# Moving the load of u in a state-space stage: from the start of its own batch to right behind the outputs that free its buffer

## The chip, the cores and the metric

The kernel runs on one core of a Trainium2 chip. The metric is the device time of one execution in microseconds (us); lower is better. Times of a kernel before and after a change are compared as ratios with an interval.

The core has a matrix engine (TensorE, PE in the profile; its weight loads are listed as PEld), a vector engine (VectorE, DVE), a scalar engine (ScalarE, ACT), GpSimd (POOL), and SyncE (SP), which here only issues transfers to and from memory. Each engine works through its own list of instructions in the order in which the list was written. An instruction that has to wait for another engine holds up everything behind it in its own list.

## The reference, cut to what matters

The reference is a two-layer trunk over 1024 time steps and 1024 channels, all in float32. Layer 0 computes one projection of the normalised input and splits it into `u`, a gate, `q`, `k`, `v` and a second gate. `u` goes through a diagonal complex state-space layer ("S5"), `q`, `k`, `v` through chunkwise retention; both are gated, joined and projected back. Layer 1 is a gated convolution module. The change lies in the state-space layer, which in the reference is, for each of 64 groups of 16 channels and 64 states:

```
bu_re = einsum('tbgh,gnh->tbgn', u_c, bb_re)
bu_im = einsum('tbgh,gnh->tbgn', u_c, bb_im)
pr, pim, zr, zi = lax.associative_scan(
    _complex_affine_combine, (a_r, a_i, bu_re, bu_im), axis=0)
...
y = (einsum('tbgn,ghn->tbgh', xr, cre)
     - einsum('tbgn,ghn->tbgh', xi, cim)
     + dsk * u_c)
```

## The kernel before, in words

The input projection is done in blocks of 128 output channels. Eight blocks (`u_block`) make `u` and write it to memory in a layout that puts 8 neighbouring time steps and 16 channels on the 128 partitions. Sixteen blocks (`gate_block`, nb = 8 to 23) make the two gates; each is two halves of 24 matmuls of 128x512 (L200 to L202), scaled out of PSUM by VectorE (L393), passed through Silu by ScalarE (L394) and stored (L397).

The state-space layer is cut into 8 batches, B = 0 to 7, of 8 groups each, which are interleaved with the 16 gate blocks, two blocks to a batch. This document writes v(B), y(B), U(B) and so on for the instructions of one batch. A batch consists of:

- `s5_tables(B)`: GpSimd makes tables (18 operations, L766 to L768). For B > 1 it calls `s5_w2(B)`, which loads four tables, PTr, PTi, BTr and BTi (256 KB each, L799 and L802), and lets VectorE make the two weight tiles W2r and W2i of the batch from them, in six operations (L806 to L811; the last of W2r is L810, of W2i L811). For B = 0 and 1 the weights come from TensorE transposes that ScalarE copies (L859). Each of these tiles has one buffer.
- `s5_states(B)`: loads `U`, the batch's part of u, 512 KB (L850); TensorE multiplies it with W2r and W2i (L868, called v here); VectorE turns the result, runs two scans (L883) and makes the states S (L894, L895). Beside that, TensorE and ScalarE make a kernel matrix (kp L902 and L903, Kg L905 and L906, its transpose kt L908) which goes through memory (k_d L912, Wd L915) into the weights W1 (L917).
- `s5_out(B)`: TensorE multiplies W1 with U (L932) and W3 with S (L938, both called y here); ScalarE copies the result (L942), which is stored (y_d, L944).

`U` has two buffers, so the load of batch B+1 has to wait until the L932 matmuls of batch B-1 have read theirs. As the code is written, `s5_out(B - 1)` comes between the two gate blocks of batch B, and `s5_tables(B + 1)` after the second one.

The transfers are issued by SyncE in one list. A line of `s5_w2` ties the four table loads to the load of U: `issue_after(x)` adds an edge that keeps every instruction of the block, on the engine of x, behind x in that engine's list.

```
with self.tc.issue_after(self.u_load.ins):
    for c, (pt, bt) in enumerate(((ptr, btr), (pti, bti))):
        nc.sync.dma_start(pt[:]..., ...)
        nc.sync.dma_start(bt[:]..., ...)
```

`self.u_load` is whichever load of U was written last when `s5_w2` is called. Before the change, at `s5_tables(B + 1)` that is the load of U(B).

The order of each engine's list is set by a planner when the kernel is built. It walks a timeline that it reckons with its own durations, and gives each engine, among the instructions that are ready by that reckoning, the one that comes first in the code. An instruction can thus go far ahead of its place in the code (the loads of U(0) and U(1) are issued one behind the other), but the list that results is fixed, whatever the chip then does.

Of the kernel before, what the change touches and what calls it, by code (L numbers as in the profile page):

```python
# [11 lines left out]
F32 = mybir.dt.float32  # L12
# [7 lines left out]
P = 128  # L20
# [50 lines left out]
class Trunk:  # L71
# [191 lines left out]
    def layer0_front(self, st):  # L263
        tc, nc, A = self.tc, self.nc, self.A
# [36 lines left out]
        for kb in range(KB):  # L301
            t = xt[kb] = ev.tile([P, T], F32, name=f"x_{kb}", tag="xin", bufs=8)
            g = self.vec(V_NG0, kb)
# [66 lines left out]
        def u_block(nb):  # L370
            ut = uv.tile([P, 8, P], F32, name=f"ut_{nb}", tag="ut", bufs=2)

            def evac(h, ps):
                r = self.R[:, h * HALF:(h + 1) * HALF]
                o = ut[:, ::-1, h * 64:(h + 1) * 64].rearrange("p j (a m) -> p j a m", a=LANES)

                with self.tc.issue_after(self.u_evac[0].ins) if nb == 1 else nullcontext():
                    self.u_evac[nb] = nc.vector.tensor_tensor(
                        o, ps[:].rearrange("p (m j a) -> p j a m", j=8, a=LANES),
                        r.rearrange("p (a m j) -> p j a m", j=8, a=LANES), op=ALU.mult)  # L380
            if nb < 3:
                for h in range(2):
                    evac(h, (u01 + [u2])[nb][h])
            else:
                scaled(nb, self.wnext(f"u{nb}"), f"u{nb}", evac)
            nc.sync.dma_start(self.u_d[nb].rearrange("j h g m -> (h g) j m"), ut[:])

        def gate_block(nb, w, dst):
            gt = uv.tile([P, T], F32, name=f"gt_{nb}", tag="ut", bufs=2)

            def evac(h, ps):
                c = slice(h * HALF, (h + 1) * HALF)
                nc.vector.tensor_tensor(nat(gt[:, c]), un(ps[:]), nat(self.R[:, c]), op=ALU.mult)  # L393
                nc.scalar.activation(gt[:, c], gt[:, c], AF.Silu)  # L394
            scaled(nb, w, f"g{nb}", evac)
            k = nb % 8
            nc.sync.dma_start(dst[k * P:(k + 1) * P], gt[:])  # L397
# [12 lines left out]
        self.s5 = self.pool("s5w", 1, stack=st)  # L410
        for nb in range(5, 8):
            u_block(nb)
        self.s5_tab, self.s5_back, self.s5_last = {}, {}, None
        self.s5_turned()
        self.s5_tables(0)
        for nb in range(8, 24):
            B = (nb - 8) // 2
            if nb % 2 == 0:
                self.s5_states(B)
            gate_block(nb, self.wnext(f"g{nb}"), self.gs_d if nb < 16 else self.gr_d)  # L420
            if nb % 2 == 0 and B:
                self.s5_out(B - 1)
            if nb % 2 and B < 7:
                self.s5_tables(B + 1)
        self.s5_out(7)
# [388 lines left out]
    def s5_tables(self, B):  # L814
# [24 lines left out]
            nc.scalar.mul(R8[:, q, :], self.m01[:], self.r8[:, 4 * B + q:4 * B + q + 1])  # L839
        self.s5_tab[B] = Mr, Mi, W3, Tc, Ts, R8, self.s5_w2(B) if B > 1 else None  # L840

    def s5_states(self, B):
        nc, w = self.nc, self.s5
        gp, v = nc.gpsimd, nc.vector
        q0 = 4 * B
        Mr, Mi, W3, Tc, Ts, R8, W2 = self.s5_tab.pop(B)


        U = w.tile([P, 8, P], F32, name=f"U_{B}", tag="U", bufs=2)
        self.u_load = nc.sync.dma_start(U[:], self.u_d[B].rearrange("j h g m -> (j h) g m"))  # L850


        first, W2 = W2 is None, W2 or []
        for nm, M in (("r", Mr), ("i", Mi)) if first else ():
            ps = self.bank(f"w2{nm}_{B}")
            for q in range(4):
                nc.tensor.transpose(ps[:, q * P:(q + 1) * P], M[:, q, :], self.ident[:])
            t = self.big(f"W2{nm}_{B}", f"W2{nm}", 1)
            nc.scalar.copy(t[:].rearrange("p q n -> p (q n)"), ps[:])  # L859
            W2.append(t)  # L860

        V = []
        for c in range(2):
            ps = self.bank(f"v{c}_{B}")
            for q in range(4):
                for g2 in range(2):
                    r = slice(64 * g2, 64 * g2 + 64)
                    nc.tensor.matmul(ps[r, q * P:(q + 1) * P], W2[c][:, q, r], U[:, 2 * q + g2, :],  # L868
                                     start=True, stop=True)
            V.append(ps)  # L870
        fl = lambda t: t[:].rearrange("p q n -> p (q n)")

        tc, ts = fl(Tc), fl(Ts)
        vr, vi = V[0][:], V[1][:]
        t2, t4 = (fl(self.big(f"m{i}_{B}", "tmpV", 4)) for i in range(2))
        v.tensor_tensor(t2, vi, ts, op=ALU.mult)
        v.tensor_tensor(t4, vr, ts, op=ALU.mult)
        v.tensor_tensor(vr, vr, tc, op=ALU.mult)
        v.tensor_tensor(vi, vi, tc, op=ALU.mult)
        v.tensor_tensor(vr, vr, t2, op=ALU.add)  # L880
        v.tensor_tensor(vi, vi, t4, op=ALU.subtract)
        for z in (vr, vi):
            v.tensor_tensor_scan(z, fl(R8), z, 0.0, op0=ALU.mult, op1=ALU.add)  # L883

        S = w.tile([P, 2, 4, P], F32, name=f"S_{B}", tag="S", bufs=1)
        c1 = lambda t: t[:, :, 1:P]
        c0 = lambda t: t[:, :, 0:P - 1]
        zr, zi = (z.rearrange("p (q n) -> p q n", q=4) for z in (vr, vi))
        t2, t3 = (self.big(f"d{i}_{B}", "tmpV", 4) for i in range(2))
        v.tensor_tensor(c0(t2), c0(zi), c0(Ts), op=ALU.mult)  # L890
        v.tensor_tensor(c0(t3), c0(zr), c0(Ts), op=ALU.mult)
        v.tensor_tensor(c0(zr), c0(zr), c0(Tc), op=ALU.mult)
        v.tensor_tensor(c0(zi), c0(zi), c0(Tc), op=ALU.mult)
        v.tensor_tensor(c1(S[:, 0]), c0(zr), c0(t2), op=ALU.subtract)  # L894
        v.tensor_tensor(c1(S[:, 1]), c0(zi), c0(t3), op=ALU.add)  # L895
        v.memset(S[:].rearrange("p c q m -> p (c q) m")[:, :, 0:1], 0.0)


        kp = self.bank(f"kp_{B}")
        for q in range(4):  # L900
            o = kp[q * 32:(q + 1) * 32, :P]
            nc.tensor.matmul(o, self.cbr[:, q0 + q, :], Mr[:, q, :], start=True, stop=False)  # L902
            nc.tensor.matmul(o, self.cbni[:, q0 + q, :], Mi[:, q, :], start=False, stop=True)  # L903
        Kg = w.tile([P, P], F32, name=f"Kg_{B}", tag="Kg", bufs=1)
        nc.scalar.copy(Kg[:, 16:], kp[:, 16:P])  # L905
        v.tensor_tensor(Kg[:, :16], kp[:, :16], self.dd[:, B, :], op=ALU.add)  # L906
        kp = self.bank(f"kt_{B}")
        nc.tensor.transpose(kp[:, :P], Kg[:], self.ident[:])  # L908
        Kt = w.tile([P, P], F32, name=f"Kt_{B}", tag="Kg", bufs=1)
        nc.scalar.copy(Kt[:], kp[:, :P])  # L910

        nc.sync.dma_start(self.k_d[B, 112:], Kt[:])  # L912
        Wd = w.tile([P, 8, P], F32, name=f"Wd_{B}", tag="yb", bufs=1)
        kd = self.k_d[B]
        nc.sync.dma_start(Wd[:], bass.AP(tensor=kd.tensor, offset=kd.offset, ap=[[P, P], [16 * P, 8], [1, P]]))  # L915
        W1 = w.tile([P, 8, P], F32, name=f"W1_{B}", tag="W1", bufs=1)
        nc.scalar.copy(W1[:].rearrange("p g (i h) -> p i g h", i=8), Wd[:].rearrange("p i (g h) -> p i g h", g=8))  # L917
        self.s5_back[B] = U, W1, W3, S

    def s5_out(self, B):  # L920


        nc = self.nc
        U, W1, W3, S = self.s5_back.pop(B)
        yb = self.s5.tile([P, 8, P], F32, name=f"yb_{B}", tag="yb", bufs=1)
# [3 lines left out]
        def products():  # L929
            for q in range(4):  # L930
                for g2 in range(2):
                    yield nc.tensor.matmul(ps[g2][:, cols(q)], W1[:, 2 * q + g2, :], U[:, 2 * q + g2, :],  # L932
                                           start=q == 0, stop=False)
# [993 lines left out]
```

## Time and profile before

| | |
|---|---|
| median of 3 runs | 1144.9 us (1144.89 to 1146.61) |
| the profiled execution, its time | 1147.62 us |
| the profiled execution, span from first to last instruction | 1145.8 us |
| mean granted TensorE clock in it | 0.994 |
| state-space stage with the gate blocks | about 83 to 320 us of the span |
| U loads issued | 83.3 (two), 139.2, 170.6, 198.3, 227.7, 255.5, 283.2 us |
| v starts, B = 0 to 7 | 102.2, 126.6, 149.4, 176.9, 204.4, 232.5, 260.1, 289.1 us |
| W2i finished by VectorE, B = 2 to 7 | 146.0, 168.9, 196.6, 226.0, 253.8, 281.5 us |

A row of the timeline gives the start and the duration in us, the engine (with a q for an instruction that issues a transfer), the line of the code, the operation, the tile written and the tiles read, and how many instructions are merged into the row. In brackets stands how long the engine had been idle before it and what ended that. A row of the waits gives who waited for whom, the total, the number of times and the longest. A row of the windows gives a stretch of the span and, for each engine, how long it was busy in it. Matmuls of the gate blocks start 0.216 us apart when nothing holds them up; their duration of 0.38 us overlaps the next.

### The profile page before, as it was taken

The page shows a single profiled execution, that of the slowest core. Times are in us where ns is not written, and L with a number is a line of the kernel's source. Part 1 is how long each engine was busy: PE and PEld are TensorE (multiplying, and loading weights), DVE is VectorE, ACT ScalarE, POOL GpSimd, SP SyncE. Part 2 cuts the span into 40 slices and gives each one's busy share as a digit, 9 for nine tenths or more (in the row PEclk, how much of TensorE's full clock was granted, in tenths as well). Part 3 has the DMA queues.
Part 4 walks back from the last instruction along what each step waited for, and adds up shares of the span by engine and source line. Part 5 has one row for each costly group of instructions (what it writes and reads, how often), then busy time and mean ns, then how long its engine had stood idle before and what let it go on. Part 6 is the DMA issues. An engine that isn't in the chain of part 4 may idle for free.

```text
span 1145.8 us, 17197 instructions
## 1 busy us (share of the span) xinstructions
PE 1123.9 (98%) x6286; PEld 983.4 (86%) x6286; DVE 853.5 (74%) x1464; ACT 488.2 (43%) x719; POOL 657.7 (57%) x448
## 2 busy tenths in 40 slices
PE   9999999999999999999999999999999999999997
PEld 7888888888887888999887888888888888888787
DVE  6975798888417369596669632599999899999844
ACT  6423232223223321414446423545545676444674
POOL 2059999999235445333475111589544568678563
PEclk9999999999999999999999999999999999999999
DMA  9345355555487766858998998666778655357865
GB/s 352 113 129 159 128 166 177 162 175 177 154 256 247 285 199 211 297 182 308 382 375 295 321 321 285 191 232 203 247 249 298 238 177 173 120 188 248 287 226 193
DMA packets 117638, 261.46 MB, mean 228 GB/s; under 512 B 10673, under 2 KB 42289, under 8 KB 116913
## 3 DMA queue, kind: packets, MB, share of 16 engines
q1 hardware_dynamic: 117552, 260.36, 67.5%
q8 instruction: 49, 0.80, 0.3%
q14 instruction: 37, 0.30, 0.1%
HBM read 181.48 MB, written 74.65 MB: 224 GB/s over the span
## 4 chain that ended last, share of the span: by engine, by line
PE 34%; DVE 8%; DMA 7%; issue 2%; POOL 2%; ACT 1%; SPq 1%; POOLq 0%; ACTq 0%; DVEq 0%
DVE cv L1534 5%; PE mm_wo L202 5%; PE mm_wo L201 5%; PE mm_wo L200 5%; PE mm_b L201 2%; PE mm_b L202 2%; PE mm_b L200 2%; PE mm_a L202 2%; PE mm_a L201 2%; PE mm_a L200 2%; PE mm_oc L202 2%; PE mm_oc L201 1%; PE mm_oc L200 1%; DMA wf_glu<-w_glu 1%; DMA t_d<-th 1%
## 5 line engine op out<-in xcount | busy, mean ns | idle before, releaser
L1534 DVE SCALAR_TENSOR_TENSOR cv<-u,convw,cv 128x512 f32<-128x512 f32 x398 | 273.0, 749 | 6.6 <-ACT cv L1513 4.6
L1507 POOL TENSOR_TENSOR tp<-tp,tp 128x512 f32<-128x512 f32 x64 | 83.2, 1299 | 33.7 <-ACT tp L1506 32.7
L200 PE MATMUL mm_g<-xh,wh_g 128*128 128x512 f32 x256 | 98.9, 386 | 0.0
L201 PE MATMUL mm_g<-xl,wh_g 128*128 128x512 f32 x256 | 97.3, 380 | 0.0
L202 PE MATMUL mm_g<-xh,wl_g 128*128 128x512 f32 x256 | 97.2, 380 | 0.0
L437 POOL TENSOR_TENSOR s1q<-s1q,s1q 128x512 f32<-128x512 f32 x12 | 17.6, 1466 | 79.8 <-ACT s1q L432 79.8
L1506 ACT ACTIVATE tp<-u,convw 128x512 f32<-128x512 f32 x64 | 45.4, 718 | 35.5 <-POOL tp L1507 34.8
L200 PEld LDWEIGHTS mm_g<-xh,wh_g 128*128 128x128 f32 x256 | 48.4, 189 | 8.6 <-issue 1.2
L202 PEld LDWEIGHTS mm_g<-xh,wl_g 128*128 128x128 f32 x256 | 48.4, 189 | 6.9
L201 PEld LDWEIGHTS mm_g<-xl,wh_g 128*128 128x128 f32 x256 | 48.4, 189 | 6.8 <-issue 0.4
L190 POOL TENSOR_TENSOR wl_v<-wf_v,wh_v 128x1024 fp32r<-128x1024 f32 x12 | 31.0, 2593 | 36.4 <-ACT wh_v L189 36.4
L190 POOL TENSOR_TENSOR wl_glu<-wf_glu,wh_glu 128x1024 fp32r<-128x1024 f32 x14 | 34.3, 2447 | 29.9 <-ACT wh_glu L189 29.9
L200 PE MATMUL mm_oc<-zh,wh_woc 128*128 128x512 f32 (+1 forms) x144 | 51.3, 367 | 0.0
L202 PE MATMUL mm_oc<-zh,wl_woc 128*128 128x512 f32 (+1 forms) x144 | 51.0, 357 | 0.1
L201 PE MATMUL mm_oc<-zl,wh_woc 128*128 128x512 f32 (+1 forms) x144 | 51.1, 356 | 0.0
L201 PE MATMUL mm_u<-xl,wh_u 128*128 128x512 f32 x128 | 48.4, 381 | 0.7 <-DVE xl L316 0.7
L200 PE MATMUL mm_wo<-ysh,wh_wos 128*128 128x512 f32 x128 | 48.9, 382 | 0.0
L200 PE MATMUL mm_g<-h1h,wh_cg 128*128 128x512 f32 x128 | 48.9, 382 | 0.0
L201 PE MATMUL mm_b<-h1l,wh_cb 128*128 128x512 f32 x128 | 48.7, 381 | 0.1
L202 PE MATMUL mm_b<-h1h,wl_cb 128*128 128x512 f32 x128 | 48.7, 380 | 0.0
L201 PE MATMUL mm_wo<-ysl,wh_wos 128*128 128x512 f32 x128 | 48.5, 379 | 0.0
L202 PE MATMUL mm_wo<-ysh,wl_wos 128*128 128x512 f32 x128 | 48.5, 379 | 0.0
(526 smaller groups left out, 3622.9 us busy)
## 6 DMA issues: line engine op xcount, KB each, us to landing
wf_g<-w_ab SPq DMA_DIRECT2D x16, 512.0 KB
wf_wos<-w_out SPq DMA_DIRECT2D x16, 512.0 KB
wf_wor<-w_out SPq DMA_DIRECT2D x16, 512.0 KB
wf_cb<-w_c SPq DMA_DIRECT2D x16, 512.0 KB
wf_ca<-w_c SPq DMA_DIRECT2D x16, 512.0 KB
wf_woc<-w_out_c SPq DMA_DIRECT2D x16, 512.0 KB
wf_v<-w_v SPq DMA_DIRECT2D x12, 512.0 KB
wf_cg<-w_c SPq DMA_DIRECT2D x11, 512.0 KB
```

The lines of the kernel that those rows point to most:

```text
L190: self.low_made = lo[i].tensor_tensor(wl[:].rearrange(fl)[:, c], wf[:, c], h.bitcast(F32), op=ALU.subtract)
L200: nc.tensor.matmul(ps, wh[:, kb, :], xh, start=start, stop=False, **more)
L201: nc.tensor.matmul(ps, wh[:, kb, :], xl, start=False, stop=False, **more)
L202: self.last_mm = nc.tensor.matmul(ps, wl[:, kb, :], xh, start=False, stop=stop, **more)
L437: nc.gpsimd.tensor_tensor(a, a, sq[:], op=ALU.add)
L1506: nc.scalar.mul(sk[:], u[:, k:k + HALF], cw[:, nb, k:k + 1])
L1507: gp.tensor_tensor(s0[:], s0[:], sk[:], op=ALU.add)
L1534: v.scalar_tensor_tensor(dst[:], *tap, accs_[i][:], op0=ALU.mult, op1=ALU.add)
```

## The change

The load of U leaves `s5_states` and becomes a function of its own. For B = 0 and 1 it is called at the start of the batch, as before. For B = 2 to 7 it is called right behind `s5_out(B - 2)`, one gate block and one `s5_tables` earlier in the code. The buffers, the transfer and all computation stay the same. Because `self.u_load` is now set earlier, `s5_w2(B)` finds the load of U(B) in it, where it found that of U(B-1) before.

```
-        self.s5_tab, self.s5_back, self.s5_last = {}, {}, None
+        self.s5_tab, self.s5_back, self.s5_last, self.s5_us = {}, {}, None, {}
         self.s5_turned()
         self.s5_tables(0)
         for nb in range(8, 24):
             B = (nb - 8) // 2
             if nb % 2 == 0:
+                if B < 2:
+                    self.s5_load(B)
                 self.s5_states(B)
             gate_block(nb, self.wnext(f"g{nb}"), self.gs_d if nb < 16 else self.gr_d)
             if nb % 2 == 0 and B:
                 self.s5_out(B - 1)
+                if B < 7:
+                    self.s5_load(B + 1)
             if nb % 2 and B < 7:
                 self.s5_tables(B + 1)
         self.s5_out(7)
...
+    def s5_load(self, B):
+
+        U = self.s5_us[B] = self.s5.tile([P, 8, P], F32, name=f"U_{B}", tag="U", bufs=2)
+        self.u_load = self.nc.sync.dma_start(U[:], self.u_d[B].rearrange("j h g m -> (j h) g m"))
+
     def s5_states(self, B):
...
-        U = w.tile([P, 8, P], F32, name=f"U_{B}", tag="U", bufs=2)
-        self.u_load = nc.sync.dma_start(U[:], self.u_d[B].rearrange("j h g m -> (j h) g m"))
-
+        U = self.s5_us.pop(B)
```

## The prediction

> **What bounds the kernel now.** I read the busy times of the page first, then the windows of the state-space stage, the waits of TensorE in it, and the timeline of one batch on each engine.
>
> ```profile
> PE 1123.9 (98%) x6286; PEld 983.4 (86%) x6286; DVE 853.5 (74%) x1464; ACT 488.2 (43%) x719; POOL 657.7 (57%) x448
> ```
> ```profile
> 210.00:240.00 30.00, 29.37 (x203) 25.60 (x202) 25.30 (x31) 8.11 (x15) 29.53 (x21) 1.00 0.52 162
> 270.00:300.00 30.00, 28.57 (x200) 24.88 (x199) 24.87 (x33) 8.38 (x16) 21.30 (x15) 1.00 0.43 142
> ```
> ```profile
> PE v L868 <- ACT gt L394: 1.4, 1, 1.4
> PE v L868 <- DMA U<-u_d: 0.6, 1, 0.6
> ```
>
> TensorE is the bound: 98% of the span, and in the stage (columns: PE, PEld, DVE, ACT, POOL busy) it lacks 0.6 us in one window and 1.4 us in another. These are its only two waits there, both at v. What they cost stands in its timeline.
>
> ```profile
> 204.04 0.38 PE L202 MATMUL mm_g<-xh,wl_g 128*128 128x512 f32 x1
> 204.35 1.09 PE L868 MATMUL v<-U,W2r 128*64 128x128 f32 x16
> 217.42 1.95 PE L932 MATMUL y<-U,W 128*128 128x128 f32 x16
> 231.53 0.38 PE L202 MATMUL mm_g<-xh,wl_g 128*128 128x512 f32 x1
> 232.53 1.09 PE L868 MATMUL v<-U,W2r 128*64 128x128 f32 x16 [0.63 <-DMA U<-u_d]
> 287.27 0.38 PE L202 MATMUL mm_g<-xh,wl_g 128*128 128x512 f32 x1
> 289.08 1.09 PE L868 MATMUL v<-U,W2r 128*64 128x128 f32 x16 [1.43 <-ACT gt L394]
> ```
>
> A step from a gate matmul into v takes 0.31 us without a wait (204.04 to 204.35). At v(5) it takes 1.00, so 0.69 lost; at v(7) 1.81, so 1.50 lost. The row names ScalarE for v(7), but v reads nothing of gt. U(7) was issued 5.9 us before:
>
> ```profile
> 283.21 0.38 SPq L850 DMA_DIRECT2D U<-u_d  x1
> ```
>
> U(5), issued at 227.71 (its row is below), was followed by its v after 4.8 us, so I take v(7) to wait for U(7) as well. Together **2.2 us**, all that an earlier U can give TensorE directly.
>
> **The change part by part.** It adds no transfer and no arithmetic: eight U loads before and after, costed at nothing in themselves. Two things move: U in SyncE's list, and through `u_load` the four table loads of W2.
>
> *U.* SyncE's list around U(5):
>
> ```profile
> 221.02 0.37 SPq L915 DMA_DIRECT2D Wd<-k_d  x1
> 227.30 0.32 SPq L397 DMA_DIRECT2D gr_d<-gt  x1
> 227.71 0.39 SPq L850 DMA_DIRECT2D U<-u_d  x1
> 228.15 0.67 SPq L799 DMA_DIRECT2D PTr<-pt_d  x1
> ...
> 230.11 0.59 SPq L802 DMA_DIRECT2D BTi<-bt_d  x1
> ```
>
> The first y matmuls of batch 3 (217.42 + 1.95) free U's buffer at 219.37. U(5) goes at 227.71, 8.3 us later, behind a gate's store. In the new list it may pass that store and Wd. What it gives v is at most the 2.2 us above. The store that it passes costs nothing: nobody waits for it in this stage; Wd, 0.4 us of issue later, has until W1 is read by y, 20 us on. At the other end U passes nothing and stays at 227.7, and the gain is 0.
>
> *The table loads.* Today the loads at 228.15 to 230.11 are those of W2(6), behind U(5). Afterwards W2(5)'s must stand behind U(5) and W2(6)'s behind U(6), one batch later; they sit in SyncE's list behind a wait for y. The W2 chain of batch 5, on VectorE, with two rows of the next batch that show when tables arrive:
>
> ```profile
> 207.32 1.60 DVE L806 TENSOR_TENSOR W2r<-PTr,BTr 128x512 f32<-128x512 f32 x1
> 211.23 1.62 DVE L807 TENSOR_TENSOR W2i<-PTr,BTi 128x512 f32<-128x512 f32 x1
> 214.06 1.66 DVE L808 TENSOR_TENSOR PTr<-PTi,BTi 128x512 f32<-128x512 f32 x1
> 217.88 1.77 DVE L809 TENSOR_TENSOR PTi<-PTi,BTr 128x512 f32<-128x512 f32 x1
> 219.57 1.87 DVE L810 TENSOR_TENSOR W2r<-W2r,PTr 128x512 f32<-128x512 f32 x1
> 224.34 1.67 DVE L811 TENSOR_TENSOR W2i<-W2i,PTi 128x512 f32<-128x512 f32 x1
> 236.81 1.20 DVE L806 TENSOR_TENSOR W2r<-PTr,BTr 128x512 f32<-128x512 f32 x1 [2.74 <-DMA BTr<-bt_d]
> 240.69 1.25 DVE L807 TENSOR_TENSOR W2i<-PTr,BTi 128x512 f32<-128x512 f32 x1 [0.28 <-DMA BTi<-bt_d]
> 127.83 0.69 DVE L806 TENSOR_TENSOR W2r<-PTr,BTr 128x512 f32<-128x512 f32 x1 [4.47 <-PE v L868]
> ```
>
> W2(5) is finished at 226.0, 6.5 us ahead of v(5), spread over 18.7 us among other work. That cover is gone. The new path, from 219.37: U issued after 2 us (between 0 and the 8.3 of today); BTi there 10.5 us later (today 13.0, from 227.71 to 240.69, with a weight load and a y store behind it in the queue, which the earlier place leaves out; U alone took 4.8, from 227.71 to v at 232.53, and the four issues 3.0 more, so no less than 7.8); the five operations left, 8.6 less 0.4 of overlap; one more for a gate's scaling in between. Sum 2 + 10.5 + 8.2 + 1 = 21.7: W2i at about 241, where the gate block in front of v(5) makes room at 231.8 (231.53 and the step of 0.31). So it comes **9 us late**; with 0, 7.8, 8.2 and 0 it is 4 us, with 8.3, 13.0, 8.2 and 1 it is 18. I stay near the middle, as SyncE may still meet another wait in front of U, and as the loads that follow U's today (a weight block and the y store, 1 MB) would mostly come later. Batch 2 loses most cover: its tables are loaded at about 100 us today, and U(2) goes at 139.
>
> Behind the waiting table loads in SyncE's list stand a weight load for a later gate block, Wd and the y store; the weights are asked for two blocks ahead, 2 x 48 x 0.216 = 21 us, so I cost them at nothing, and 2 us a batch if that lead were gone. Behind L806, which will wait for BTr, stand the scalings of the gates (L393); three PSUM banks of 24 x 0.216 = 5.2 us each let TensorE go on for 10 us, so nothing for them either. Who does wait is v.
>
> Not all of that is a stall, as the planner can put gate matmuls in front. It did so where W2 came last, in batch 1:
>
> ```profile
> 122.86 0.58 ACT L859 COPY W2i<-w2i 128x512 f32<-128x512 f32 x1
> ```
> ```profile
> 126.64 1.09 PE L868 MATMUL v<-U,W2r 128*64 128x128 f32 x16
> ```
>
> v(1) stands inside a gate block, 3.2 us behind the end of its weights (123.44). So the planner leaves a margin over its own reckoning. How that reckoning stands to the chip shows at kt, which also goes in as soon as it is ready, behind L906:
>
> ```profile
> 205.32 2.08 DVE L190 TENSOR_TENSOR wl_g<-wf_g,wh_g 128x1024 fp32r<-128x1024 f32 x1 [0.17 <-ACT wh_g L189]
> ...
> 212.78 0.16 DVE L906 TENSOR_TENSOR Kg<-kp,s_s_dd 128x16 f32<-128x16 f32 x1
> ...
> 293.55 0.16 DVE L906 TENSOR_TENSOR Kg<-kp,s_s_dd 128x16 f32<-128x16 f32 x1
> ```
> ```profile
> 214.07 0.27 PE L908 MATMUL kt<-ident,Kg 128*128 128x128 f32 x1
> 297.72 0.27 PE L908 MATMUL kt<-ident,Kg 128*128 128x128 f32 x1
> ```
>
> In batch 7, with no W2 ahead of it, kt has 4.0 us of margin (293.71 to 297.72); in batch 4, behind L190, L806 and L807, 1.1 us. The 2.9 us lost are about what these three took beyond an undisturbed pace (1.60 and 1.62 against 0.69 in the row at 127.83, with GpSimd busy 98% of the window). So the planner reckons W2 operations at the undisturbed 0.69 us.
>
> [...]
>
> Stall of one batch: the five operations' unreckoned part, 8.2 - 3.4 = 4.8; transfers later than reckoned, 1.6 (the mean of 2.74 that VectorE stood for BTr above and of 0.69 and 1.50 that v stood for U); less the margin, 3.4 (3.2 to 4.0, nearer the first, which is v's own). That is **3.0 us**, between 0 (margin covers all) and 9 (v stays where it is). Batches 2 to 7: 6 x 3.0 = 18.0. The 2.2 us of waits for U are swallowed, since W2 now comes last. GpSimd's tables, Kg, W1 and S keep cover: v 9 us later ends VectorE's part of batch 7 at about 309, before y(7) at 316.47.
>
> ```profile
> 316.47 1.95 PE L932 MATMUL y<-U,W 128*128 128x128 f32 x16
> ```
>
> Sum: 18.0 - 2.2 = **+15.8 us**. Against the profiled execution, 1147.62, that is 1163.4; against the median of 1144.9, 2.7 below it, **1160.7**. After the stage TensorE stays the bound (98% of the whole span), so I let the shift pass through to the end.
>
> **The rivals.** *No stall (faster or the same).* The planner sets each v 22 us or more behind the y that frees U; gate matmuls fill the time, and only the waits for U vanish: 1144.9 - 2.2 = 1142.7. For it: v(0) and v(1) do stand inside gate blocks. Against: the margins at kt, used up by contention. What decides is where v stands in TensorE's list: each us that it stands short of 21.7 behind the end of y's first matmuls costs 6 us.
>
> *v stays in front of its gate block.* Then the full 9 us is waited for, six times: 54 - 2.2 gives 1196.7. The same comes out if v moves but U does not, and stays behind the gate's store, which adds 6 us to the path (8.3 in place of 2): the change then does not do what it says, and the stall is 3.0 + 6.3. For it: v(2) to v(7) all stand exactly there today. Against: that is where they were ready in time.
>
> *Stalls that also slow the clock.* After one wait the trace has matmuls 0.43 us apart:
>
> ```profile
> 359.50 0.48 PE L1137 MATMUL mm_v<-wl_v,xh 128*128 128x512 f32 x1 [2.32 <-POOL wl_v L190]
> ```
> ```profile
> 361.20:364.20 3.00, 3.00 (x8) 2.32 (x7) 3.00 (x2) 1.06 (x2) 3.00 (x2) 0.50 0.45 186
> ```
>
> Seven of them at granted clock 0.50 lost 7 x 0.21 = 1.5 us. Six times that adds 9: 1169.7. Against: the shorter waits at v were followed by full speed.
>
> [...]
>
> **How the numbers follow.** Stalls of 1 to 5.5 us a batch: 0.47. With the slower clock: 0.10. v in front of its block: 0.15. No stall: 0.28, of which I give 0.17 to faster and 0.11 to the same, since 2.2 us is just the 0.2% that a measurement of this kernel can tell from no change. Slower 0.72. The range runs from 1142.5, no stall, to 1188, most of the way to the worst; the likeliest case alone is 1149 to 1176.
>
> **What would show it.** Right: table loads of W2(B) behind U(B) in SyncE's list; waits at v in batches 2 to 7 that VectorE's L810 or L811 ends; v inside gate blocks; U issued within some 2 us of y. Wrong: v without waits, W2 operations near 0.69 us, or waits that another stage gives back.

## The result, and the profile after

The changed kernel takes 1172.9 us (median of 4 runs, 1170.4 to 1176.3) against 1145.8 us for the kernel before on the same chip: a ratio of 1.0232, 95% interval 1.021 to 1.0254. It is slower by some 27 us; 15.8 were forecast. The profiled execution took 1174.35 us, its span is 1172.6 us.

The busy times of the changed kernel, from its page:

```profile
PE 1127.9 (96%) x6286; PEld 988.2 (84%) x6286; DVE 832.8 (71%) x1464; ACT 488.7 (42%) x719; POOL 641.0 (55%) x448
```

The work is the same and TensorE is still the bound, but it is now idle for 4% of the span, where it was 2%. The waits of TensorE in the state-space stage (who waited for whom, us in total, times, longest) show where:

```profile
PE v L875 <- issue: 22.4, 6, 7.0
PE v L875 <- ACT gt L394: 0.5, 3, 0.2
```

Six waits, one at each of v(2) to v(7); the lines have moved, v is L875 now. Before, two waits at v came to 2.0 us. The same stretch of both kernels (PE, PEld, DVE, ACT, POOL busy, then granted clock, DMA share, GB/s), first before, then after:

```profile
83.00:346.00 263.00, 260.94 (x1749) 227.94 (x1748) 177.59 (x219) 77.28 (x135) 219.19 (x155) 1.00 0.55 174
```
```profile
83.00:346.00 263.00, 240.16 (x1595) 209.21 (x1594) 153.24 (x213) 72.12 (x130) 190.35 (x148) 0.97 0.44 143
```

TensorE lacks 2.1 us there before and 22.8 after, and the granted clock falls from 1.00 to 0.97. Both count: y(7), the end of the stage, starts 28.3 us later than the 316.47 of before.

```profile
344.74 1.95 PE L939 MATMUL y<-U,W 128*128 128x128 f32 x16
```

Steps from the last gate matmul into v lose 22.8 us (7.0, 4.3, 3.2, 3.0, 2.5 and 2.8), of which 2.2 were lost before already: 20.6. The other 7.7 us lie behind the waits. Narrow windows of the changed kernel show the granted clock at 0.50 for 17.1 us of the stage (from 155.7, 189.8, 254.7 and 285.4 us on); TensorE was idle in 3.6 of these, and in the other 13.5 it lost half its pace, 6.7 us (from the first half of v to the second it takes 1.73 us there at v(3), and 0.92 at v(4) of the kernel before, at full clock). The second halves of v(4), v(5) and v(7), which wait for W2i, come 0.3 us late each: 1.0 us. Behind the stage both kernels take about as long (829.3 us before, 827.9 after, from the start of y(7) to the end of the span), so nothing was given back.

How one wait comes about is seen at v(4). SyncE, VectorE and TensorE of the changed kernel, in the timeline:

```profile
206.28 0.32 SPq L397 DMA_DIRECT2D gs_d<-gt  x1
206.69 1.10 SPq L849 DMA_DIRECT2D U<-u_d  x1
207.84 0.60 SPq L803 DMA_DIRECT2D PTr<-pt_d  x1
208.50 0.58 SPq L806 DMA_DIRECT2D BTr<-bt_d  x1
209.12 0.58 SPq L803 DMA_DIRECT2D PTi<-pt_d  x1
209.75 0.58 SPq L806 DMA_DIRECT2D BTi<-bt_d  x1
```
```profile
215.07 1.72 DVE L810 TENSOR_TENSOR W2r<-PTr,BTr 128x512 f32<-128x512 f32 x1 [5.07 <-DMA BTr<-bt_d]
219.43 0.69 DVE L811 TENSOR_TENSOR W2i<-PTr,BTi 128x512 f32<-128x512 f32 x1 [2.65 <-DMA BTi<-bt_d]
220.16 0.69 DVE L812 TENSOR_TENSOR PTr<-PTi,BTi 128x512 f32<-128x512 f32 x1
220.88 0.69 DVE L813 TENSOR_TENSOR PTi<-PTi,BTr 128x512 f32<-128x512 f32 x1
221.49 0.68 DVE L814 TENSOR_TENSOR W2r<-W2r,PTr 128x512 f32<-128x512 f32 x1
222.69 0.68 DVE L815 TENSOR_TENSOR W2i<-W2i,PTi 128x512 f32<-128x512 f32 x1
```
```profile
204.69 1.95 PE L939 MATMUL y<-U,W 128*128 128x128 f32 x16
218.80 0.38 PE L202 MATMUL mm_g<-xh,wl_g 128*128 128x512 f32 x1
222.28 1.09 PE L875 MATMUL v<-U,W2r 128*64 128x128 f32 x16 [3.10 <-issue]
223.52 1.09 PE L875 MATMUL v<-U,W2i 128*64 128x128 f32 x16 [0.15 <-ACT gt L394]
```

y(2) reads its U until 206.64; U(4) goes at 206.69, BTi is there at 219.43, W2r is finished at 222.17, and v starts at 222.28. The gate matmuls last only until 218.80 (with the step of 0.31, v could have started at 219.11). The rows name "issue" as what ended the wait, but v starts 0.11 us behind W2r's end. What stands behind v in TensorE's list comes behind it here too, kp at 224.55 and the next gate matmul at 225.14. The path from y to the end of W2 takes 16.7 us; TensorE has 12.5 us of work in its list between the same y and v.

In batches 3 to 7 v stands where it stood before, in front of its gate block and 48 gate matmuls behind y. Batch 2 differs: 14 matmuls (3.0 us) of v's own gate block stand in front of it (the last is of L201, where a half ends with L202), and it still waits 7.0 us.

```profile
151.69 0.38 PE L201 MATMUL mm_g<-xl,wh_g 128*128 128x512 f32 x1
159.04 1.33 PE L875 MATMUL v<-U,W2r 128*64 128x128 f32 x10 [6.97 <-issue]
```

### The profile page after: what moved, and what is told of

Read it like the earlier page. It is cut to its first block, busy times and chain, and to the rows that moved or that the text cites. A ratio compares the mean times of both kernels' runs of the same rounds, so it can differ in the third digit from the quotient of the medians.

```text
span 1172.6 us, 17178 instructions
## 1 busy us (share of the span) xinstructions
PE 1127.9 (96%) x6286; PEld 988.2 (84%) x6286; DVE 832.8 (71%) x1464; ACT 488.7 (42%) x719; POOL 641.0 (55%) x448
## 4 chain that ended last, share of the span: by engine, by line
PE 64%; DMA 13%; DVE 11%; issue 4%; ACT 3%; POOL 3%; SPq 2%; POOLq 0%; DVEq 0%; ACTq 0%
DVE cv L1541 5%; PE mm_wo L202 4%; PE mm_wo L200 4%; PE mm_wo L201 4%; PE mm_g L200 3%; PE mm_g L201 3%; PE mm_g L202 3%; DMA BTi<-bt_d 3%; PE mm_b L201 2%; PE mm_b L202 2%; PE mm_b L200 2%; PE mm_a L201 2%; PE mm_a L202 2%; PE mm_a L200 2%; PE v L875 2%
## 5 line engine op out<-in xcount | busy, mean ns | idle before, releaser
L201 PE MATMUL mm_g<-xl,wh_g 128*128 128x512 f32 x256 | 98.0, 383 | 0.0
L202 PE MATMUL mm_g<-xh,wl_g 128*128 128x512 f32 x256 | 97.4, 381 | 0.0
L394 ACT ACTIVATE gt<-gt 128x512 f32<-128x512 f32 x32 | 20.1, 629 | 92.7 <-DVE gt L393 92.6
L201 PEld LDWEIGHTS mm_g<-xl,wh_g 128*128 128x128 f32 x256 | 48.6, 190 | 7.0 <-issue 0.4
L202 PEld LDWEIGHTS mm_g<-xh,wl_g 128*128 128x128 f32 x256 | 48.6, 190 | 7.0 <-issue 0.2
L202 PE MATMUL mm_oc<-zh,wl_woc 128*128 128x512 f32 (+1 forms) x144 | 51.1, 357 | 0.1
L201 PE MATMUL mm_oc<-zl,wh_woc 128*128 128x512 f32 (+1 forms) x144 | 51.1, 356 | 0.0
L201 PE MATMUL mm_u<-xl,wh_u 128*128 128x512 f32 x128 | 48.5, 381 | 0.7 <-DVE xl L316 0.7
L201 PE MATMUL mm_b<-h1l,wh_cb 128*128 128x512 f32 x128 | 48.8, 381 | 0.1
L202 PE MATMUL mm_b<-h1h,wl_cb 128*128 128x512 f32 x128 | 48.6, 380 | 0.0
L201 PE MATMUL mm_wo<-ysl,wh_wos 128*128 128x512 f32 x128 | 48.6, 379 | 0.0
```

The costliest lines, as they stand in the source:

```text
L201: nc.tensor.matmul(ps, wh[:, kb, :], xl, start=False, stop=False, **more)
L202: self.last_mm = nc.tensor.matmul(ps, wl[:, kb, :], xh, start=False, stop=stop, **more)
```

## The experiments

The theory to test: the edge that ties the table loads to U puts them behind y(B-2), and v, which keeps its place in TensorE's list in all batches but batch 2, waits for what the path is too long. The rivals are that U's own place does the harm, that the W2 operations are slowed by GpSimd, and that the half clock is the larger part. All ratios are to the kernel before on the same chip.

**Each half of the edit by itself.** First U is loaded where the change loads it, but the tables of a batch stay tied to the U of the batch before:

```
-        with self.tc.issue_after(self.u_load.ins):
+        with self.tc.issue_after(self.u_was.ins):
...
-        self.u_load = self.nc.sync.dma_start(U[:], ...)
+        self.u_was, self.u_load = getattr(self, "u_load", None), self.nc.sync.dma_start(U[:], ...)
```

> The load of U is moved as in the change, but the table loads of W2(B) stay tied to U(B-1), as before the change. Theory (the 27 us come from the table loads, which stand behind U(B) and so behind y(B-2)): W2 is finished before v again, TensorE does not wait for it, and the time is 1142.5 to 1146.5 us; it is at the low end if U now also comes early enough to spare v(5) and v(7) their 2.2 us. Rival (the moved U, its traffic or the new order of the list itself is what costs): 1160 us or more, with v still waiting some 3 us in each batch.

Measured: 1143.7 us, 1.0001 (0.998 to 1.0021). The waits of TensorE in the stage are gone but for 0.3 us at kt and

```profile
PE v L875 <- DMA U<-u_d: 0.5, 2, 0.4
```

SyncE's timeline shows that U did not get earlier. Batch 3's y frees its buffer at 218.35, and U(5) goes 8.3 us later, behind the same gate store as before:

```profile
219.94 0.37 SPq L922 DMA_DIRECT2D Wd<-k_d  x1
226.19 0.32 SPq L397 DMA_DIRECT2D gr_d<-gt  x1
226.61 0.38 SPq L849 DMA_DIRECT2D U<-u_d  x1
```

The order Wd, gate store, U, tables is that of the kernel before, and so is the whole list of the stage. Moving U in the code moved nothing in the list that is issued; it neither gains nor costs anything that can be measured.

Then the tables alone: the kernel before, with the tables of batch B tied behind the y store of batch B-2 instead of U(B-1).

```
-        with self.tc.issue_after(self.u_load.ins):
+        with self.tc.issue_after(self.y_store.ins):
...
-        nc.sync.dma_start(self.y_d[B]..., yb[:])
+        self.y_store = nc.sync.dma_start(self.y_d[B]..., yb[:])
```

> The other half: the kernel before, with U loaded where it was, but the table loads of W2(B) tied behind the y store of batch B-2. Theory: the tables come later still than in the changed kernel (today that store is issued 12.2 us behind the end of y's first matmuls), W2 is late in every batch from 2 on, and the time is 1175 to 1220 us; if the planner moves v into its gate block, by some 20 to 30 matmuls, the lower end. Rival (the place of U is what costs, not that of the tables): 1143 to 1148 us.

Measured: 1187.8 us, 1.0391 (1.0347 to 1.0435). Its waits in the stage:

```profile
PE v L868 <- issue: 25.1, 5, 6.4
PE v L868 <- ACT gt L394: 5.7, 1, 5.7
```

Late tables by themselves make the kernel slower, by more than the whole change, as the y store is later than U: BTi of one batch goes at 221.35, 12.1 us behind the U load at 209.25. Here the planner did put 16 to 33 gate matmuls of v's own block in front of v in every batch from 2 on; in the changed kernel it put 14 in batch 2 and none in the others.

The third kernel has U as in the change and no edge at all:

```
-        with self.tc.issue_after(self.u_load.ins):
+        with nullcontext():
```

> The changed kernel with the order edge between U and the four table loads left out; U moves as in the changed kernel. Theory that the edge alone carries the loss: 1142 to 1147. Rival, part of the loss comes with U's own place: 1150 or more.

Measured: 1150.8 us, 1.0056 (1.0036 to 1.0076). Without the edge 6 us are left of the 27, which is the time that the rival gave. The trace puts most of it at one v, v(3), with a wait of 4.1 us and 6.8 us of half clock from there on:

```profile
PE v L875 <- DMA U<-u_d: 4.1, 1, 4.1
```
```profile
173.49 0.60 SPq L803 DMA_DIRECT2D PTi<-pt_d  x1
174.76 0.31 SPq L397 DMA_DIRECT2D gs_d<-gt  x1
175.16 0.38 SPq L849 DMA_DIRECT2D U<-u_d  x1
```

Untied, the tables of the next batch go ahead of U, each waiting for VectorE to have read its buffer, and U(3) stands behind them: 9.3 us behind the end of y(1)'s U part (165.82). So the tie to the U of the batch before keeps the tables out of U's way; it is its move to the U of the same batch that does the harm.

**The path started earlier.** The changed kernel with three buffers for U, so that U(B), and the tables with it, need not wait for y(B-2). The room came from tmpV, whose four buffers became two (one of its four places is shown); a control run has only that cut.

```
-        U = self.s5_us[B] = self.s5.tile([P, 8, P], F32, name=f"U_{B}", tag="U", bufs=2)
+        U = self.s5_us[B] = self.s5.tile([P, 8, P], F32, name=f"U_{B}", tag="U", bufs=3)
...
-        t2, t3 = (self.big(f"d{i}_{B}", "tmpV", 4) for i in range(2))
+        t2, t3 = (self.big(f"d{i}_{B}", "tmpV", 2) for i in range(2))
```

> The changed kernel with three buffers for U in place of two, so that the load of U(B) has no y(B-2) to wait for; to make room, the tiles of VectorE's turn (tag tmpV) have two buffers in place of four. The table loads stay tied behind U(B). Theory (the tie costs only because U(B) waits for y): U and the tables go early, no wait for W2 at v, 1142 to 1148 us. Rival (one batch's transfers together, or the order itself, are what is too slow): 1160 us or more.

> Control for the run with three U buffers, which paid for the third one with two of the four buffers of tmpV: the changed kernel with only that cut. If the third U buffer brought the gain there, this stays at the changed kernel's 1170 to 1177; if the cut of tmpV did it (GpSimd and VectorE slowed to another order), it comes near 1144.

Measured: 1144.0 us, 1.0007 (0.9987 to 1.0026) with the third buffer; 1174.0 us, 1.0245 (1.02 to 1.029) for the control. With three buffers no wait at v is left in the stage, at an unchanged edge:

```profile
PE kt L915 <- DVE Kg L913: 0.9, 2, 0.7
```

So the loss needs both: the tables behind U, and U behind y. Even with U early, nothing beyond the kernel before is gained.

**v later.** The changed kernel, with the states of batches 2 to 7 written behind the first gate block of their batch instead of ahead of it. v then has 68 gate matmuls between itself and y in TensorE's list, where it had 48.

```
-                self.s5_states(B)
+                if B < 2:
+                    self.s5_states(B)
             gate_block(nb, ...)
+            if nb % 2 == 0 and B > 1:
+                self.s5_states(B)
```

> The changed kernel with the states of batches 2 to 7 written behind their first gate block instead of in front of it, so that v stands some 10 us later in TensorE's list and everything in front of W2 is as in the change. Theory (W2 comes 3 to 7 us after v's place in the list, and nothing else is wrong): the waits at v are gone, 1142 to 1148 us, up to 5 us more if the states of the last batch now end late. Rival (the path from y to v is too long for the period, or SyncE's list holds other work up): 1160 us or more.

Measured: 1159.2 us, 1.0137 (1.0101 to 1.0173). The loss is halved, not removed:

```profile
PE v L878 <- ACT gt L394: 10.6, 4, 3.4
PE v L878 <- DVE W2i L818: 2.1, 3, 0.7
PE v L878 <- issue: 0.2, 1, 0.2
```

y moved back together with v, so the room grew by 20 x 0.216 = 4.3 us only, and the path grew too: to 18.7 us in batch 6 (from 265.23, where y(4) lets go of U, to 283.96, where W2i is finished), and to 20 to 22 us in batches 3, 4, 5 and 7, where U went only 3.6 to 4.9 us behind y, directly behind Wd in SyncE's list. v(2) has 94 gate matmuls behind y and waits for nothing. The expected time had counted on more room, and on a path that stays as it is.

**The W2 operations beside GpSimd.** In the changed kernel five of the six of batch 4 take 0.69 us, in the kernel before none of batch 5's did. GpSimd's timeline gives the reason:

```profile
216.19 1.56 POOL L770 TENSOR_TENSOR o<-s_bbi,s_pi 128x512 f32<-128x512 f32 x1
225.34 1.26 POOL L771 TENSOR_TENSOR Mr<-s_bbr,s_pr 128x512 f32<-128x512 f32 x1 [7.59 <-PE kp L910]
```

Mr has one buffer, its last reader is kp, kp stands right behind v in TensorE's list, and v waits: so GpSimd stands still just while the W2 operations run. To undo this, kp is written ahead of v:

```
+        kp = self.bank(f"kp_{B}")
+        for q in range(4): ...
         V = []
...
-        kp = self.bank(f"kp_{B}")
-        for q in range(4): ...
```

> The four kp products of a batch are written ahead of its v, so that Mr and Mi, which have one buffer, come free before v has waited, and GpSimd can go on beside the W2 operations. Theory that an idle GpSimd shortens the path in the changed kernel (W2 operations 0.69 us there against 1.4 to 1.7 where GpSimd works): the four operations behind BTi take 3 to 4 us longer, v starts that much later in up to six batches, and the time rises by 6 to 24 us, 1179 to 1197. Rival, the transfers alone set the time of W2: 1168 to 1177, as the changed kernel. If kp's place only matters for what runs behind v, less than that: GpSimd's help is earlier and nothing in the stage is lost, 1165 to 1172.

Measured: 1179.3 us, 1.031 (1.0289 to 1.0332), at the lower end of what the first theory gave, and above the changed kernel's interval. VectorE's rows of batch 4 in this kernel:

```profile
220.81 0.69 DVE L812 TENSOR_TENSOR PTr<-PTi,BTi 128x512 f32<-128x512 f32 x1
221.53 1.64 DVE L813 TENSOR_TENSOR PTi<-PTi,BTr 128x512 f32<-128x512 f32 x1
223.09 1.75 DVE L814 TENSOR_TENSOR W2r<-W2r,PTr 128x512 f32<-128x512 f32 x1
225.36 0.98 DVE L815 TENSOR_TENSOR W2i<-W2i,PTi 128x512 f32<-128x512 f32 x1
```

GpSimd writes Mr again at 221.52, and from there on the operations take 0.98 to 1.75 us. That makes the way from U's issue to v 0.8 us longer on the mean of six batches; y(7) starts at 349.89, 5.2 us later than in the changed kernel. The time by itself is weak evidence, as a second measurement of the changed kernel, below, gave 1.0261 (1.0235 to 1.0287); the rows are the stronger one. The slow rows come back with GpSimd at work, and that is the reason why the forecast's contended price did not apply: waiting for v, GpSimd let VectorE alone (0.69 us a row).

**The clock.** The changed kernel, with idle matmuls of 512 columns in front of v from batch 2 on, so that TensorE works while it waits. Fourteen of them (3.0 us) first:

```
+            for _ in range(14 if B > 1 and c == 0 else 0):
+                nc.tensor.matmul(ps[:], self.ones_r[:], mv(self.xs[0][0][0][:]), start=True, stop=True)
```

> Fourteen matmuls of 512 columns, on data that lie ready, are added in front of v in batches 2 to 7, into a bank that v overwrites; their results are thrown away. They take 14 x 0.216 = 3.0 us of each wait of 2.5 to 7.0 us and cost nothing as long as the wait is longer. Theory that about 8 us of the loss is half clock behind the waits: the waits that TensorE is idle shrink below 4 us, the granted clock in the stage goes from 0.97 to 1.00, and the time falls to 1164 to 1169. Rival, the clock is no part of the loss: 1171 to 1177.

Then thirty in batch 2 and fourteen elsewhere, beside the changed kernel once more:

> As the run with fourteen idle matmuls in front of v, but thirty of them in batch 2, where 6 us of wait were left. Theory that the half clock behind the waits is a part of the loss: TensorE is never idle for more than 1 us in front of v, the granted clock is 1.00 through the stage, the stage ends 23 us later than before instead of 28, and the time is 4 to 7 us under the changed kernel's (1166 to 1169). Rival, no part: within 1.5 us of the changed kernel.

> The changed kernel once more, beside the two that follow and on the same chip, so that they can be compared with it directly: 1170 to 1176.

Measured: 1169.3 us, 1.0209 (1.0175 to 1.0243), for the first, just above what the theory gave, and the interval doesn't tell it from the changed kernel; 1168.1 us, 1.019 (1.0166 to 1.0214), for the second, and 1177.3 us, 1.0261 (1.0235 to 1.0287), for the changed kernel beside it. The stage in the first, in the same columns as above:

```profile
83.00:346.00 263.00, 257.00 (x1725) 224.66 (x1724) 154.83 (x213) 73.00 (x132) 192.75 (x148) 0.99 0.45 148
```

The clock is up from 0.97 to 0.99, and y(7) starts at 339.74, 5.0 us earlier than in the changed kernel, with the path from y to v about as long as ever; one wait of 6.0 us, at v(2), was left. In the second kernel y(7) starts at 341.59, only 2.5 us earlier than the 344.09 of the changed kernel beside it, though the times differ by 9.2; two waits at W2r (4.2 us together) were left, and the clock in the stage was 0.99, so the theory's time came true, but not its clock of 1.00 nor its waits under 1 us, and the stage ended 25.1 us late where it said 23. Both figures are too low for the clock's part, because the idle matmuls also took the place of the 14 gate matmuls in front of v(2): from y(0) to y(1) it takes 37.5 and 37.9 us with them, 35.8 and 35.6 without. So the clock is a part of the loss: 6.7 us by the count of half clock above, of which 5.0 and 2.5 us were given back on balance in the stages' traces. The two executions beside each other differ by another 6.2 us behind the stage, up to 3.4 of it by half clock (13.7 us of it against 6.8); the rest was not traced to anything.

**The bytes.** The changed kernel, with BTr and BTi loaded for batch 2 only and read again in the later batches.

```
-                nc.sync.dma_start(bt[:].rearrange("p q n -> p (q n)"), ...)
+                if B == 2:
+                    nc.sync.dma_start(bt[:].rearrange("p q n -> p (q n)"), ...)
```

> Two of the four tables (BTr, BTi) are loaded for batch 2 only and read again in batches 3 to 7, whose results are therefore of wrong data; the vector operations, the edge behind U and all else are the changed kernel's. 0.5 MB of 1.5 MB is gone between y and W2. Theory that the transfers (2.2 us for each table of 256 KB, by the 4.4 us between the landings of BTr and BTi) set when W2 is ready: the path from U's issue to v falls from 15.6 us to 11 to 12, which is about the room that the gate matmuls leave; the waits at v fall from 3 to 4.5 us to 0 to 0.5 in batches 3 to 7, and the time to 1148 to 1156 (batch 2 keeps its wait of 7 us and some half clock). Rival, the length is a fixed delay of the loads and not their bytes: waits of 2 us and more stay, 1163 or more.

Measured: 1163.3 us, 1.014 (1.011 to 1.017), at the edge of what the rival gave and well above the theory's 1148 to 1156. TensorE's waits in the stage:

```profile
PE v L879 <- issue: 14.8, 6, 6.7
```

In batches 3 to 7 the way from U's issue to v takes 13.3 us on the mean, against 15.5 in the changed kernel beside it: 2.3 us less where 4.4 were expected. In batch 4 the last table now is PTi:

```profile
205.30 1.50 SPq L853 DMA_DIRECT2D U<-u_d  x1
...
207.51 0.58 SPq L806 DMA_DIRECT2D PTi<-pt_d  x1
```
```profile
215.64 1.17 DVE L816 TENSOR_TENSOR PTr<-PTi,BTi 128x512 f32<-128x512 f32 x1 [1.57 <-DMA PTi<-pt_d]
```

It is there 10.3 us behind U's issue, 2.4 us sooner than BTi above (12.7). So the bytes count, but a third of them less shortens the loads by a fifth only; what holds the rest was not separated (a weight load and the y store follow directly in the queue, in both kernels). Part of what was won went elsewhere: in batch 3 four of the operations took 1.48 to 1.64 us and v came 15.4 us behind U, as in the changed kernel, and in batches 5 to 7 U itself went 1.5 us behind y.

## Why the prediction was right, and where its steps were not

The direction, the cause and the place were right: the table loads went behind U, W2 came last, v waited in each of batches 2 to 7, the waits for U were swallowed, and nothing later gave the time back. The first three kernels show that this edge, and not U's own move, carries the loss. The forecast of +15.8 us was 11 us short of the medians' +27, and its steps hold less well than its sum. One of its signs of being wrong, W2 operations near 0.69 us, came true, and one of its signs of being right, v inside gate blocks, showed in batch 2 alone.

*"U issued after 2 us".* It took 0.05 in batches 4 to 7, 0.25 and 0.84 in 3 and 2, but not because U passed the gate's store: the store still stands directly in front of it (206.28 and 206.69). In the kernel before the store waited for a scaling that stood on VectorE behind W2i; with W2 gone from there the scaling is done before y ends:

```profile
224.34 1.67 DVE L811 TENSOR_TENSOR W2i<-W2i,PTi 128x512 f32<-128x512 f32 x1
225.93 0.68 DVE L393 TENSOR_TENSOR gt<-mm_g,R 128x512 f32<-128x512 f32 x1
```
```profile
204.89 0.69 DVE L393 TENSOR_TENSOR gt<-mm_g,R 128x512 f32<-128x512 f32 x1 [2.09 <-PE mm_g L202]
```

The first fence is the kernel before, the second the changed one. U did not stay 8.3 us behind y, though its place in the list is just what that rival said.

*"BTi there 10.5 us later".* 12.7, nearer to the 13.0 of the kernel before than to the middle; the weight load and the y store that were to come later follow directly.

*"The five operations left, 8.6 less 0.4 of overlap; one more for a gate's scaling".* 3.9 us in all (219.43 to 223.37). This is the term that was furthest off: the contended price came from rows in which GpSimd was busy for 98% of the window, and in the changed kernel GpSimd waits for the same v. The run with kp ahead of v brought 1.64 and 1.75 us back. So the rows take 0.69 us while GpSimd stands, and 1.64 and 1.75 while it works; in what way it holds them up, no run shows.

The path is thus 16.7 us and not 21.7, and v's gap at its old place 4.3 us in this batch (3.1 of it a wait, as v needs only W2r to start), not 9.

*"Less the margin, 3.4".* This step failed. In batches 3 to 7 v did not move: it stands in front of its gate block with 48 gate matmuls behind y, where the prediction had it inside, with a margin. Only in batch 2 did it move, by 14 matmuls, and with no margin. The rival "v stays in front of its gate block" thus has the right place in five batches of six, at 2.5 to 4.3 us a batch where it said 9. How the 4.2 us that are missing in batch 4 divide is an estimate: if the planner reckoned this path to fit into the 12.5 us that it left for it, and took four of them for the vector work, it left 8.5 for loads that took 12.7. By that it was 4.2 on late transfers, where the prediction put 1.6, and nothing on contention, where it put 4.8. Why v moved in batch 2, and in every batch of the kernel whose tables hang on the y store, but not in the others here, can't be read from a trace and stays open.

So 4.8 + 1.6 - 3.4 = 3.0 us a batch came near the 3.8 measured (22.8 / 6) by errors that cancel, which is luck. Batch 2, named as the one that loses most cover, did: 7.0 us.

*The clock.* The prediction left it at a rival (9 us, one chance in ten), since shorter waits had been followed by full speed (0.63 and 1.43 us, v at 1.09). The stage shows 7.7 us beyond the waits, 6.7 of them by half clock, and the idle matmuls took a part of that back. With 18.0 raised to 22.8 and the 7.7 added, less the 2.2, the sum is 28.3, the lateness of y(7).

*"Costed at nothing".* This held for U's load, the weights and Wd: in the changed kernel TensorE waits for nothing but v in the stage.

## What to carry to other kernels

Before a load is moved, look for what is tied to it: here the load moved nowhere, and four others that were ordered behind it got a batch later, onto the path to TensorE. A path is to be compared with the work that the list holds between its two ends (16.7 against 12.5 us), and a list written ahead of time does not stretch when the chip is slower than it was reckoned to be. A duration taken from a contended row holds only as long as the neighbour works (1.60 to 1.87 us before, 0.69 in the changed kernel): ask whether the new wait stops the neighbour too.

## What the runs showed of the hardware that was not expected

The granted clock does not follow the length of a wait alone. Two waits of the changed kernel, at v(5) and v(6), and what came behind them, in TensorE's timeline:

```profile
253.15 1.09 PE L875 MATMUL v<-U,W2r 128*64 128x128 f32 x16 [2.94 <-issue]
254.40 1.73 PE L875 MATMUL v<-U,W2i 128*64 128x128 f32 x16 [0.15 <-ACT gt L394]
...
285.09 1.71 PE L875 MATMUL v<-U,W2r 128*64 128x128 f32 x16 [2.45 <-issue]
```

Behind 3.10 us (v(4), above) both halves of v took 1.09 us, full speed; behind 2.94 the second half took 1.73; behind 2.45, the shortest, both were slow (1.71 and 1.99). The four stretches of half clock in the stage start 34.1, 64.9 and 30.7 us apart, which is 10, 19 and 9 steps of 3.41 us, and last one such step or, the first of them, two. In this stage they go with how busy TensorE was in the step before. Here are the steps around v(5) and around v(7), which waited 2.73 us (TensorE's busy time alone, then granted clock, DMA share, GB/s):

```profile
251.29:254.70 3.41, 1.40 (x22) 1.00 0.06 23
254.70:258.11 3.41, 3.41 (x34) 0.50 0.45 156
312.73:316.14 3.41, 1.52 (x8) 1.00 0.44 178
316.14:319.55 3.41, 2.42 (x44) 1.00 0.00 0
```

A step with 1.40 us of work was followed by half clock, one with 1.52 was not. The wait at v(6) lay within one step and left it 0.96 us of work; the longer one at v(4) was split over two, with 2.03 and 1.55. The steps ahead of the other two stretches, in the waits at v(2) and v(3), had none at all. Where the limit lies, or whether there is one, the traces do not show: behind the stage of the changed kernel a step with 1.59 us of work (from 517.52 on) was followed by half clock and one with 1.62 (from 633.58 on) was not, and in the kernel before one with 1.43 (from 357.52 on) was and one with 1.58 (from 606.70 on) was not. So where a wait falls on these steps counts beside its length: in the changed kernel the one of 2.45 us at v(6) was enough, and the one of 3.10 at v(4) was harmless.
